# A hybrid mixer and mixture-of-experts layer on one core: two expert pairs in a fixed place instead of one, gathered together in front; the order of pairs and fours; the order of the routing steps; the sort key of the fixed experts

## The chip, the core and the metric

The kernel runs on one core of one Trainium2 chip. The time is device time in microseconds for one execution, from launch to the last output. Lower is better.

## What is computed

One decoder layer for 512 tokens of 1024 features, all in float32. The first half is a mixer: one input projection (1024 to 3072), a gated short convolution on one part, block attention on the other, an output projection, and a layer norm after the residual. The second half is a mixture of 32 experts in 4 groups, two experts for each token, plus a gated per-layer embedding ("PLE"), and a second layer norm. The reference, cut to what matters here:

```python
mix = jnp.concatenate([y_conv, y_attn], axis=-1) @ w_out[i]
x = layer_norm(DEEPNORM_ALPHA * x + mix, ln1_g[i], ln1_b[i])
# routing: one group of four by softmax, then two of its eight experts
g_p, g_idx = lax.top_k(softmax(xt @ w_router_g + b_router_g), 1)
e_p, e_local = lax.top_k(softmax(e_logits_of_that_group), 2)
weights = g_p * (e_p / e_p.sum(-1, keepdims=True))
# every expert, on the tokens that chose it (D_EXPERT = 512)
hid = silu(xb @ w_gate[e]) * (xb @ w_up[e])
y = y.at[tokens].add((hid @ w_down[e]) * weight)
ple = sigmoid(x @ w_ple_gate[i]) * (p[i] @ w_ple_proj[i])
x = layer_norm(DEEPNORM_ALPHA * x + y + ple, ln2_g[i], ln2_b[i])
```

The weights of the 32 experts are 192 MiB (201 MB) of float32 in HBM. Every one of them is read once in every execution.

## The kernel before

**The front.** The kernel does the mixer with float32 split into a high and a low part, three matmuls for one product (`mm3`, lines 132 to 134). Then comes the output projection of the four tiles of 128 tokens, tt = 0 to 3. `project(tt, half, part)` is 12 matmuls of 128x512; part 1 multiplies the attention's half, part 0 the convolution's. `residual`, `stats`, `centre_row`, `finish_row` and `low_row` make the layer norm of a tile on VectorE (with two tiny steps of GpSimd for the root), and leave it as a high part `x1h` and a low part `x1l`. `turn_raw` transposes a tile for the router, `logits` makes the router's 40 columns, `route` finds each token's two experts on VectorE (`mb` marks them), `rank` counts each token's place within its expert, `select` writes 0/1 matrices of tokens against places, and `gather_first` multiplies x1h and x1l by them, which collects the first unit's tokens in `xe[0]`. `router_constants` folds the norm's gain and bias into the router's weights.

**The table.** `sort_experts` orders the experts by their number of tokens, so that the fullest stand first. It writes `table` (line 712), the row in HBM where each sorted expert's weights begin. The first NFIX experts by number are kept out of the sorting: they always stand first, so that their weights can be fetched without the table.

**The units.** The sorted experts are worked through in 12 units, by `KINDS`. A "P" unit is a pair of experts with 64 places each, and its weights are 12 pieces of 1 MiB. A "Q" unit is four experts with 32 places each and has 24 such pieces. There are 8 P and 4 Q units. For a unit, TensorE does `gate_up` for k = 0 to 7, then `swiglu` (ScalarE and VectorE), `turn_hidden` (four transpositions), `down` for f = 0 to 3; `scatter_pair` adds the result to the tokens' rows while the next unit runs. Units are put together in `GROUPS`; during the last unit of a group the next group's tokens are gathered (`gather_group`, 8 pieces). The PLE's 16 tasks are spread over units by the dictionary `PLE`.

**The slots and the queue of loads.** SBUF holds 24 slots of 1 MiB (`Slots`, first in, first out). All loads stand in one queue in a fixed order; `pump` takes a slot for the next load wherever one has been given back. All DMAs are issued by SyncE (SP), one after another, and a load's issue waits until the last reader of its slot is done; what stands behind it waits too. An entry in `closed` stops the queue: `("e", 1, 0, 0)`, the first piece of unit 1, is closed until the table is written, because that load's address comes from the table (`load_expert`, line 263 reads the table, line 266 issues; line 258 issues the loads of unit 0, whose place is fixed). Towards the end `("e", 11, 0, 10)` holds back the last two pieces until `overflow` has run; that is a branch taken when some expert has more tokens than its unit has places.

```python
def pump(reserve, ahead=99):
    while queue and slots.left() > reserve and len(loaded) < ahead and queue[0][0] not in closed:
```

## Time and profile before

| | before |
|---|---|
| median of 3 runs | 785.05 us (784.99 to 785.3) |
| the profiled execution, its own time | 784.13 us |
| its span, first to last instruction | 782.3 us |
| granted clock of TensorE, mean | 0.980 |
| PE busy / weight load busy | 744.1 us (95%) / 449.6 us (57%) |
| VectorE / ScalarE / GpSimd busy | 311.0 / 164.1 / 73.5 us |
| moved by DMA | 233.53 MB, mean 299 GB/s |

The profiled execution stands 0.9 us below the median; its time is 1.8 us more than its span. Matmuls are pipelined and their ends are modelled, so that PE's busy share says little about how much room PE has. The share of the DMA engines is a mean over stages of different kinds.

### The profile page before, as it was taken

How to read it: one execution, taken by the hardware profiler on the slowest of the kernel's cores; microseconds unless marked ns; L12 is line 12 of the kernel's file. 1: busy time of each engine (PE TensorE's matmuls, PEld its weight loads, DVE VectorE, ACT ScalarE, POOL GpSimd, SP SyncE). 2: the span in 40 equal slices, each digit the busy share in tenths (PEclk: the TensorE clock that was granted, in tenths of full speed). 3: DMA queues.
4: the chain of work that ended last, by engine and by line, in shares of the span. 5: the costliest groups of instructions: out<-in, count | busy, mean ns of one | idle time of the engine just before them, and what ended most of it. 6: DMA issues, size and time to landing. Idle time of an engine off the chain costs nothing. (4 is left out here: it accounts for less than half of the span.)

```text
span 782.3 us, 11777 instructions
## 1 busy us (share of the span) xinstructions
PE 744.1 (95%) x4404; PEld 449.6 (57%) x4404; DVE 311.0 (40%) x646; ACT 164.1 (21%) x341; POOL 73.5 (9%) x104
## 2 busy tenths in 40 slices
PE   7999999999988899899999999999999999999995
PEld 4887877888866552247344653364454634447442
DVE  3746544746467513525440224241123333203254
ACT  5545444332011120103210120110010110001023
POOL 0224245000001000000000100000010000001005
PEclk9999999999989699999999999999999999999999
DMA  8500301547243998999999999998999999999952
GB/s 312 195 1 28 135 1 55 215 163 293 83 183 140 326 373 302 411 409 405 409 408 409 409 408 410 409 356 313 409 407 408 410 408 409 409 409 409 401 191 108
DMA packets 63708, 233.53 MB, mean 299 GB/s; under 512 B 7056, under 2 KB 10784, under 8 KB 59296
## 3 DMA queue, kind: packets, MB, share of 16 engines
q1 hardware_dynamic: 63648, 232.75, 76.0%
q8 instruction: 36, 0.59, 0.3%
q14 instruction: 24, 0.20, 0.1%
HBM read 230.62 MB, written 2.10 MB: 297 GB/s over the span
## 5 line engine op out<-in xcount | busy, mean ns | idle before, releaser
L983 PE MATMUL ps_mm<-big,big 128*32 128x512 f32 (+1 forms) x1024 | 215.5, 602 | 8.5 <-DMA big<-in_w_e_dram 7.7
L983 PEld LDWEIGHTS ps_mm<-big,big 128*32 128x32 f32 (+1 forms) x1024 | 57.8, 123 | 138.4 <-issue 85.7
L132 PE MATMUL ps_mm<-big,big 128*128 128x512 f32 (+1 forms) x240 | 91.2, 380 | 3.1 <-ACT big L118 3.1
L133 PE MATMUL ps_mm<-big,big 128*128 128x512 f32 (+1 forms) x240 | 88.6, 369 | 0.2 <-DVE big L119 0.2
L134 PE MATMUL ps_mm<-big,big 128*128 128x512 f32 (+1 forms) x240 | 88.3, 368 | 0.1
L1003 PE MATMUL ps_y<-big,ht 128*32 128x512 f32 (+1 forms) x480 | 84.2, 603 | 0.2 <-DMA big<-in_w_e_dram 0.2
L1024 DVE TENSOR_TENSOR big<-big,ps_s 128x512 f32<-128x512 f32 x80 | 52.9, 684 | 69.7 <-PE ps_s L1015 69.5
L119 DVE TENSOR_TENSOR big<-big,big 128x512 fp32r<-128x512 f32 (+1 forms) x74 | 58.3, 824 | 31.4 <-ACT big L118 26.5
L1015 PE MATMUL ps_s<-big,pt 128*128 128x512 f32 x176 | 59.4, 438 | 0.5 <-DVE big L1024 0.4
L118 ACT CAST big<-big 128x512 fp32r<-128x512 f32 (+1 forms) x74 | 50.5, 726 | 38.2 <-DVE big L432 20.1
L132 PEld LDWEIGHTS ps_mm<-big,big 128*128 128x128 f32 x240 | 46.4, 193 | 17.4 <-issue 6.7
L807 PEld LDWEIGHTS ps_s<-big,big 128*128 128x128 f32 x384 | 48.8, 190 | 9.8 <-issue 6.6
L801 POOL TENSOR_TENSOR big<-big,ps 128x256 f32<-128x256 f32 x16 | 11.7, 734 | 438.4 <-DVE ps L797 351.6
L807 PE MATMUL ps_s<-big,big 128*128 128x256 f32 (+1 forms) x384 | 51.9, 284 | 0.0
L134 PEld LDWEIGHTS ps_mm<-big,big 128*128 128x128 f32 x240 | 46.1, 192 | 8.0 <-DVE big L119 0.6
L133 PEld LDWEIGHTS ps_mm<-big,big 128*128 128x128 f32 x240 | 46.2, 193 | 7.3 <-DVE big L119 0.8
L1003 PEld LDWEIGHTS ps_y<-big,ht 128*32 128x32 f32 (+1 forms) x480 | 22.0, 123 | 41.4 <-issue 36.6
L374 POOL TENSOR_SCALAR big<-big,rden 128x128 f32<-128x128 f32 (+3 forms) x32 | 39.1, 1233 | 71.0 <-DVE rden L372 71.0
L797 DVE TENSOR_TENSOR ps<-ps,ps_s 128x256 f32<-128x256 f32 x16 | 6.7, 422 | 98.1 <-ACT ps L796 98.1
L1015 PEld LDWEIGHTS ps_s<-big,pt 128*128 128x128 f32 x176 | 29.3, 192 | 26.8 <-issue 17.3
L132 PE MATMUL ps_s<-big,big 128*128 128x256 f32 x128 | 37.4, 292 | 0.2
L133 PE MATMUL ps_s<-big,big 128*128 128x256 f32 x128 | 36.1, 282 | 0.0
(249 smaller groups left out, 811.0 us busy)
## 6 DMA issues: line engine op xcount, KB each, us to landing
big<-in_w_e_dram SPq DMA_DIRECT2D x360, 512.0 KB, 10.2
big<-in_w_e_dram SPq DMA_DIRECT2D x12, 1024.0 KB, 9.9
big<-in_w_in_dram SPq DMA_DIRECT2D x11, 1024.0 KB, 6.3
big<-in_w_out_dram SPq DMA_DIRECT2D x4, 1024.0 KB, 6.0
big<-in_w_pg_dram SPq DMA_DIRECT2D x4, 1024.0 KB, 11.1
big<-in_xtok_dram SPq DMA_DIRECT2D x2, 1024.0 KB, 6.9
out_dram<-big SPq DMA_DIRECT2D x8, 256.0 KB, 2.2
big<-in_xT_dram SPq DMA_DIRECT2D x3, 512.0 KB, 8.0
```

The costliest lines, as they stand in the source:

```text
L118: nc.scalar.copy(hi, raw)
L119: nc.vector.tensor_sub(lo, raw, hi.bitcast(F32))
L132: nc.tensor.matmul(o, ah, bh, start=first, stop=False)
L133: nc.tensor.matmul(o, ah, bl, start=False, stop=False)
L134: nc.tensor.matmul(o, al, bh, start=False, stop=last)
L374: nc.gpsimd.tensor_scalar(pr[h][:, 0:ks], pr[h][:, 0:ks], rden[:, h:h + 1], None, op0=ALU.mult)
L801: nc.gpsimd.tensor_tensor(r, r, s, op=ALU.add)
L807: nc.tensor.matmul(o[:, 0:n], src[tt // 2].t[:, tt % 2, k * P:(k + 1) * P], pt(tt), start=(i == 0), stop=(i == 2 * NT - 1))
L983: nc.tensor.matmul(o[a][i * m:(i + 1) * m], x, w[:, a * FE:(a + 1) * FE], start=(k == 0), stop=(k == KD - 1))
L1003: nc.tensor.matmul(o[h][r], ht[:, f, r], w[:, h * 512:(h + 1) * 512], start=(f == 0), stop=(f == 3))
L1015: nc.tensor.matmul(o, pt[0:m, tt * P:(tt + 1) * P], y[i][0:m], start=(i == 0), stop=(i == 1))
L1024: nc.vector.tensor_add(r, r, o)
```

## The change

Two constants and a table of kinds change: `KINDS` from "PQPPQPPQPPQP" to "PPPQPQPQPQPP", `NFIX` from 2 to 4, and `GROUPS` from [0], [1,2], ... [11] to [0,1], [2,3], ... [10,11]. Units 0 and 1 (experts 0 to 3) are now fixed, so 24 pieces of 1 MiB stand in the queue before the first that needs the table. `gather_first` collects the tokens of both units at once, 256 columns instead of 128, in four PSUM banks instead of two, and in more steps. `router_constants` is cut into three steps that stand between the projections; its 32 matmuls become 8 small ones and 2 that spread the result. `rank` and `select` of tiles 0 and 1 now come after tile 2's projection. `finish_row` and `low_row` of tile 2, and `finish_row` of tile 3, come before the last `route`; ten matmuls of zeros (`keep_warm`) stand behind the gather of tiles 0 and 1. The token weights, the rest of `sort_experts` and `rank(mc)` move into unit 0. The sort key of a fixed expert now also depends on its number, so that the four keep their order. `PLE` spreads the tasks as 5, 1, 4, 1, 5 over units 5 to 9 (before 4, 1, 5, 1, 5 over units 4, 6, 7, 9, 10).

```diff
--- before.py
+++ after.py
@@ -29,13 +29,13 @@
 CAP = 64
 NBLK = T // CAP
 SMALL = 32
-KINDS = "PQPPQPPQPPQP"
+KINDS = "PPPQPQPQPQPP"
 NU = len(KINDS)
-NFIX = 2
+NFIX = 4
 NWIDE = 2 * KINDS.count("P")
 UNITS = [(2 * KINDS[:u].count("P"), 2, CAP) if v == "P" else (NWIDE + 4 * KINDS[:u].count("Q"), 4, SMALL)
          for u, v in enumerate(KINDS)]
-GROUPS = [[0]] + [list(range(u, min(u + 2, NU))) for u in range(1, NU, 2)]
+GROUPS = [[u, u + 1] for u in range(0, NU, 2)]
 NP = NE // 2
 NG = len(GROUPS)
 GROUP_OF = {u: (g, r) for g, us in enumerate(GROUPS) for r, u in enumerate(us)}
@@ -49,7 +49,7 @@
 SEL = 1024.0
 N_SLOTS = 24
 WARM = 9
-PLE = {4: 4, 6: 1, 7: 5, 9: 1, 10: 5}
+PLE = {5: 5, 6: 1, 7: 4, 8: 1, 9: 5}
 WEIGHTS = {"P": [1.5, 0, 1.5, 0] + [5, 2.5] + [0, 1, 0], "Q": [2, 2, 2, 1.5] + [3, 2] + [1, 2, 1]}
 LAST = [4, 0, 4, 0, 2, 2]
 
@@ -136,7 +136,7 @@
 
     queue = deque()
     loaded = {}
-    closed = {("ln2",), ("e", 1, 0, 0), ("e", NU - 1, 0, 10)}
+    closed = {("ln2",), ("e", NFIX // 2, 0, 0), ("e", NU - 1, 0, 10)}
 
     def pump(reserve, ahead=99):
         while queue and slots.left() > reserve and len(loaded) < ahead and queue[0][0] not in closed:
@@ -254,8 +254,8 @@
 
     def load_expert(n, j, u, t):
 
-        if n == 0:
-            nc.sync.dma_start(t, w_e[0, u])
+        if 2 * n < NFIX:
+            nc.sync.dma_start(t, w_e[n, u])
             return
         for i in range(2):
             col = UNITS[n][0] + 2 * j + i
@@ -310,7 +310,8 @@
         gp.tensor_scalar(rowv[0:NE], evec[0:NE], ROWS / 2, None, op0=ALU.mult)
         gp.tensor_tensor(rowv[0:NE], rowv[0:NE], kcol[0:NE], op=ALU.add)
         for key, e in ((kcol, evec), (krow, eiota)):
-            gp.tensor_scalar(key[0:NE], e[0:NE], float(NFIX), FIRST, op0=ALU.is_lt, op1=ALU.mult)
+            gp.tensor_scalar(key[0:NE], e[0:NE], -1.0, float(NFIX), op0=ALU.mult, op1=ALU.add)
+            gp.tensor_scalar(key[0:NE], key[0:NE], 0.0, FIRST, op0=ALU.max, op1=ALU.mult)
             gp.tensor_tensor(key[0:NE], key[0:NE], e[0:NE], op=ALU.subtract)
         gp.tensor_scalar(caps, eiota, float(NWIDE), float(CAP - SMALL), op0=ALU.is_lt, op1=ALU.mult)
         gp.tensor_scalar(caps, caps, float(SMALL), None, op0=ALU.add)
@@ -609,20 +610,25 @@
                 nc.tensor.matmul(o[h, 0:NR], turned.t[:, tt % 2, k, h], wr[:, k], start=(k == 0), stop=(k == KD - 1))
         return o
 
-    def router_constants():
+    def router_constants(step):
 
         o = ps("z")
-        nc.tensor.transpose(o[:, 0:2 * KD], lnrows[0:2 * KD], ident[0:2 * KD, 0:2 * KD])
-        nc.vector.tensor_copy(gb, o[:, 0:2 * KD])
-        o = ps("z")
-        for i in range(2):
+        if step == 0:
+            nc.tensor.transpose(o[:, 0:2 * KD], lnrows[0:2 * KD], ident[0:2 * KD, 0:2 * KD])
+            nc.vector.tensor_copy(gb, o[:, 0:2 * KD])
+        elif step == 1:
             for k in range(KD):
-                nc.tensor.matmul(o[:, i * NR:(i + 1) * NR], gb[:, i * KD + k, None].to_broadcast([P, P]), wr[:, k],
+                nc.tensor.matmul(o[0:2, 0:NR], gb.rearrange("p (i k) -> p i k", i=2)[:, :, k], wr[:, k],
                                  start=(k == 0), stop=(k == KD - 1))
-        nc.vector.tensor_tensor(wr, wr, gb[:, 0:KD, None].to_broadcast([P, KD, NR]), op=ALU.mult)
-        nc.vector.tensor_scalar(gsum, o[:, 0:NR], -1.0 / D, None, op0=ALU.mult)
-        nc.vector.tensor_tensor(wr, wr, gsum[:, None, :].to_broadcast([P, KD, NR]), op=ALU.add)
-        nc.vector.tensor_add(br, br, o[:, NR:2 * NR])
+            nc.vector.tensor_copy(gsum[0:2], o[0:2, 0:NR])
+        else:
+            for i in range(2):
+                nc.tensor.matmul(o[:, i * NR:(i + 1) * NR], ident[0:2, i:i + 1].to_broadcast([2, P]), gsum[0:2],
+                                 start=True, stop=True)
+            nc.vector.tensor_tensor(wr, wr, gb[:, 0:KD, None].to_broadcast([P, KD, NR]), op=ALU.mult)
+            nc.vector.tensor_scalar(gsum, o[:, 0:NR], -1.0 / D, None, op0=ALU.mult)
+            nc.vector.tensor_tensor(wr, wr, gsum[:, None, :].to_broadcast([P, KD, NR]), op=ALU.add)
+            nc.vector.tensor_add(br, br, o[:, NR:2 * NR])
 
     gsum, lgr = work[:, 112:112 + NR], [work[:, 112 + NR * i:112 + NR * (i + 1)] for i in (1, 2)]
     wsp = cpool.tile([P, NT, NE, 2], F32R, name="wsp")
@@ -710,7 +716,7 @@
         o2 = ps("s")
         nc.tensor.matmul(o2[0:1, 0:NE], rowv[0:NE], hot[0:NE], start=True, stop=True)
         nc.vector.tensor_copy(table[0:1], o2[0:1, 0:NE])
-        closed.discard(("e", 1, 0, 0))
+        closed.discard(("e", NFIX // 2, 0, 0))
         yield
         q = qs.rearrange("p (a t) -> p a t", a=2)
         tmp = sm("ht", [P, 4, P], bufs=1)[:, 0].rearrange("p (t e) -> p t e", t=NT)
@@ -861,22 +867,27 @@
                 nc.vector.tensor_reduce(wsl[g][r][p, 0:1], o[p, c:c + 2], axis=AX.X, op=ALU.add)
         yield 0.05
 
-    def gather_first(tts, banks2=None, ks=range(KD)):
-        o = banks2
+    def gather_first(tts, o=None, ks=range(KD), srcs=(0, 1), end=False):
         if o is None:
-            o = [ps("mm") for _ in range(2)]
+            o = [ps(v) for v in ("mm", "mm", "y", "y")]
             for b in o:
                 nc.tensor.matmul(b, zerob, onesb[:, 0:1].to_broadcast([P, 512]), start=True, stop=False)
         for k in ks:
-            d = o[k // 4][:, (k % 4) * P:(k % 4 + 1) * P]
+            d = o[k // 2][:, (k % 2) * GROUP:(k % 2 + 1) * GROUP]
             for tt in tts:
-                for s in (x1h, x1l):
-                    nc.tensor.matmul(d, s[tt // 2].t[:, tt % 2, k * P:(k + 1) * P], picks(0, 0, tt),
-                                     start=False, stop=(k % 4 == 3 and tt == NT - 1 and s is x1l))
-            if k % 4 == 3 and tts[-1] == NT - 1:
-                (nc.scalar.copy if k == 7 else nc.vector.tensor_copy)(
-                    xe[0].t[:, k - 3:k + 1, 0:P], o[k // 4].rearrange("p (k s) -> p k s", k=4))
+                for i in srcs:
+                    last = end and k % 2 and tt == tts[-1] and i == srcs[-1]
+                    nc.tensor.matmul(d, (x1h, x1l)[i][tt // 2].t[:, tt % 2, k * P:(k + 1) * P], picks(0, 0, tt, 2),
+                                     start=False, stop=bool(last))
+            if k % 2 and end:
+                (nc.scalar.copy if k % 4 == 3 else nc.vector.tensor_copy)(
+                    xe[0].t[:, k - 1:k + 1], o[k // 2].rearrange("p (k s) -> p k s", k=2))
         return o
+
+    def keep_warm(o, n):
+
+        for i in range(n):
+            nc.tensor.matmul(o[i % 4], zerob, onesb[:, 0:1].to_broadcast([P, 512]), start=False, stop=False)
 
     def gather_group(g):
 
@@ -893,9 +904,11 @@
         for half in range(2):
             project(tt, half, 1)
             piece()
+            if tt == 0:
+                router_constants(half)
+    router_constants(2)
     while parts:
         piece()
-    router_constants()
     pump(2)
     for tt in range(2):
         for half in range(2):
@@ -923,18 +936,19 @@
     pump(4)
     lg[1] = logits(1)
     route((1, lg[1]))
-    rank(mb, 0, 2, NFIX)
-    select(0, (0, 1))
     project(2, 0, 0)
     residual(2, 0)
     project(2, 1, 0)
     residual(2, 1)
     stats(2)
+    rank(mb, 0, 2, NFIX)
+    select(0, (0, 1))
     project(3, 0, 0)
     turn_raw(2, 0)
     turn_raw(2, 1)
     centre_row(2)
     residual(3, 0)
+    finish_row(2)
     project(3, 1, 0)
     slots.give(ych, ycl, *(w[j] for j in (0, 1) for w in (woh, wol)))
     pump(2)
@@ -943,28 +957,27 @@
     residual(3, 1)
     turn_raw(3, 1)
     stats(3)
-    finish_row(2)
-    first = gather_first((0, 1), None, range(4))
+    low_row(2)
+    first = gather_first((0, 1), None, range(2))
     lg[3] = logits(3)
     centre_row(3)
+    finish_row(3)
     route((2, lg[2]), (3, lg[3]))
-    gather_first((0, 1), first, range(4, KD))
+    gather_first((0, 1), first, range(2, KD))
+    keep_warm(first, 10)
     rank(mb, 2, NT, NFIX)
     select(0, (2, 3))
     steps = sort_experts()
-    for _ in range(3):
-        next(steps)
-    low_row(2)
-    finish_row(3)
+    next(steps)
     low_row(3)
+    gather_first((2,), first)
+    next(steps)
+    next(steps)
     slots.give(ln1t, turned)
     pump(0)
-    gather_first((2, 3), first)
+    gather_first((3,), first, srcs=(0,))
+    gather_first((3,), first, srcs=(1,), end=True)
     weights = token_weights()
-    next(weights)
-    next(steps)
-    rank(mc, 0, NT, NE)
-    next(weights)
 
 
     def place(t, cols, n, cap):
@@ -1243,10 +1256,16 @@
                 add(7.7 if len(GROUPS[g + 1]) > 1 else 5.3, gather_group(g + 1))
             if k > 0:
                 chore()
-            if n == 0 and k == 2:
+            if n == 0 and k == 0:
+                next(weights)
+                next(steps)
+            if n == 0 and k == 1:
+                rank(mc, 0, NT, NE)
+                next(weights)
+            if n == 0 and k == 4:
                 late[0] = group_weights(0)
                 next(late[0])
-            if r == 0 and k == 4:
+            if r == 0 and k == 6:
                 for _ in late.pop(g):
                     pass
             if n == 2 and k == 6:
```

Three places show how the rows move. The first is the queue of SP's DMAs at the point where the table is first read; `big` is a slot, `in_w_e_dram` the experts' weights, 128x2048 a piece of 1 MiB. Before:

```order
L258 DMA big_2084<-in_w_e_dram 128x2048
L258 DMA big_2086<-in_w_e_dram 128x2048
L263 TENSOR_LOAD table
L263 ISA x2
L266 ISA
L266 DMA big_2253<-in_w_e_dram 128x1024
```

And of the change:

```order
L258 DMA big_2402<-in_w_e_dram 128x2048
L258 DMA big_2420<-in_w_e_dram 128x2048
L263 TENSOR_LOAD table
L263 ISA x2
L266 ISA
L266 DMA big_2426<-in_w_e_dram 128x1024
```

The read of the table stood behind 12 pieces of line 258 and now stands behind 24; nothing but such pieces lies between the 12th and the 24th.

The second place is VectorE where tile 2's projection ends. Line 655 (661 in the change) is the last step of tile 1's `route`, lines 687 to 830 (693 to 836) are `rank` and `select` of tiles 0 and 1, line 561 (562) is tile 2's residual, line 566 (567) its `stats`, line 572 (573) its `centre_row`. Before:

```order
L655 COPY lgs<-ps 128x4
L687 SCALAR_TENSOR_TENSOR rm<-mb,ps_s 128x2x2
L689 TENSOR_SCALAR rmb<-rm 128x2x2
L830 TENSOR_TENSOR big_2005<-cs,rm 128x128 x2
L561 SCALAR_TENSOR_TENSOR big_1581<-big_1581,ps_mm 128x512
L562 BN_STATS st<-big_1581 128x6
```

And of the change:

```order
L563 BN_STATS st<-big_1583 128x6
L567 BN_AGGR mv<-st 128x2
L693 SCALAR_TENSOR_TENSOR rm<-mb,ps_s 128x2x4
L695 TENSOR_SCALAR rmb<-rm 128x2x4
L836 TENSOR_TENSOR big_2038<-cs,rm 128x128 x4
L573 SCALAR_TENSOR_TENSOR big_1583<-big_1583,mv,big_1664 128x1024
L562 SCALAR_TENSOR_TENSOR big_1583<-big_1583,ps_y 128x512
```

`rank` and `select` stood between tile 1's `route` and tile 2's residual, and now stand behind tile 2's statistics; on PE the matmuls of `rank` (lines 685 and 686 of before) move in the same way from ahead of `project(2, 0, 0)` to behind `project(2, 1, 0)`.

The third place is VectorE at the end of the front. Lines 699 to 712 (705 to 718) are `sort_experts` up to the table, line 584 (585) is `low_row`, line 580 (581) `finish_row`, line 877 (883) the copy of the gathered tokens into `xe`. Before:

```order
L701 TENSOR_SCALAR gt<-ps,kc 32x32
L707 COPY pc<-ps_s 32x1
L708 TENSOR_SCALAR ps<-cs,pc 32x32
L712 CAST table<-ps_s 1x32
L584 TENSOR_TENSOR big_2125<-big_1581,big_2124 128x1024
L580 SCALAR_TENSOR_TENSOR big_1581<-big_1581,rs,big_1662 128x1024
L584 TENSOR_TENSOR big_2125<-big_1581,big_2124 128x1024
L877 COPY big_2003<-ps_mm 128x4x128
```

And of the change:

```order
L707 TENSOR_SCALAR gt<-ps,kc 32x32
L585 TENSOR_TENSOR big_2072<-big_1583,big_2071 128x1024
L713 COPY pc<-ps_s 32x1
L714 TENSOR_SCALAR ps<-cs,pc 32x32
L718 CAST table<-ps_s 1x32
L883 COPY big_2035<-ps_mm 128x512
L883 COPY big_2035<-ps_y 128x512
```

Three large steps stood between the table and the copy: `low_row(2)`, `finish_row(3)` and `low_row(3)`. Now `low_row(3)` alone is left, and it stands ahead of the table's last steps; the other two are done before the last `route`.

## Rows read from the trace of the kernel before

**Rows 1.** The page's transfer rate in 40 equal slices of 19.56 us.

```profile
GB/s 312 195 1 28 135 1 55 215 163 293 83 183 140 326 373 302 411 409 405 409 408 409 409 408 410 409 356 313 409 407 408 410 408 409 409 409 409 401 191 108
```

**Rows 2.** Windows: us; PE, PEld, DVE, ACT, POOL busy (count); clock; DMA; GB/s.

```profile
226.00:243.00 17.00, 15.71 (x87) 12.86 (x88) 8.53 (x21) 1.67 (x3) 0.74 (x2) 0.81 0.76 308
243.00:255.50 12.50, 8.06 (x105) 6.98 (x100) 10.01 (x44) 1.69 (x3) 2.59 (x2) 0.90 0.22 85
255.50:266.00 10.50, 8.67 (x44) 7.46 (x46) 5.20 (x19) 1.78 (x4) 0.29 (x1) 0.50 0.96 305
290.00:310.00 20.00, 20.00 (x144) 6.09 (x140) 4.99 (x12) 1.49 (x4) 0.00 (x0) 1.00 0.75 268
310.00:500.00 190.00, 182.79 (x1068) 87.68 (x1068) 67.73 (x134) 25.04 (x48) 2.93 (x4) 0.99 1.03 409
500.00:541.00 41.00, 40.80 (x236) 22.20 (x232) 13.91 (x25) 6.42 (x13) 0.73 (x1) 1.00 0.87 337
740.00:758.00 18.00, 17.44 (x91) 7.70 (x89) 7.67 (x16) 2.14 (x4) 0.00 (x0) 1.00 0.69 245
```

**Rows 3.** What SP's DMA queue waits for: line, releaser, total us, times, longest.

```profile
SPq L266 <- DMA big<-in_w_e_dram: 189.3, 253, 2.5
SPq L258 <- DVE big L584: 40.6, 1, 40.6
SPq L258 <- PE ps_y L134: 14.7, 1, 14.7
SPq L263 <- DVE table L712: 11.1, 1, 11.1
SPq L1047 <- SPq L1047: 9.9, 4, 6.9
```

**Rows 4.** Timeline of SP: start, us, line, tile, count.

```profile
224.66 17.32 SPq L258 DMA_DIRECT2D big<-in_w_e_dram  x6
254.10 45.93 SPq L266 DMA_DIRECT2D big<-in_w_e_dram  x34
```

**Rows 5.** Two windows of the front, columns as before.

```profile
195.90:202.70 6.80, 6.80 (x26) 5.53 (x27) 2.58 (x6) 0.00 (x0) 0.00 (x0) 0.81 0.53 219
254.00:264.50 10.50, 7.65 (x43) 7.24 (x43) 5.40 (x14) 1.25 (x2) 0.00 (x0) 0.50 0.84 255
```

**Rows 6.** Timeline of PE in the front; brackets: idle before, and its releaser.

```profile
191.89 4.20 PE L620 MATMUL ps_z<-pt,gb 128*128 128x40 f32 x32 [0.27 <-DVE gb L616]
...
227.29 0.16 PE L686 MATMUL ps_s<-mb,marks 128*128 128x2 bf16 x1 [3.90 <-DVE mb L654]
...
246.22 1.13 PE L609 MATMUL ps_z<-pt,big 128*64 128x40 f32 x32
...
254.27 0.48 PE L874 MATMUL ps_mm<-big,big 128*128 128x128 f32 x1 [1.15 <-DVE big L584]
256.54 0.47 PE L874 MATMUL ps_mm<-big,big 128*128 128x128 f32 x1 [1.79 <-ACT big L581]
```

**Rows 7.** Timeline of VectorE at the end of the front.

```profile
249.88 0.41 DVE L654 SCALAR_TENSOR_TENSOR mb<-cs,jf,hw 128x32 bf16<-128x32 f32 x2
...
252.91 0.18 DVE L712 CAST table<-ps_s 1x32 int32<-1x32 f32 x1 [0.40 <-PE ps_s L711]
253.01 1.20 DVE L584 TENSOR_TENSOR big<-big,big 128x1024 fp32r<-128x1024 f32 x1
```

**Rows 8.** Timeline of PE in the first units.

```profile
264.48 4.75 PE L983 MATMUL ps_mm<-big,big 128*64 128x512 f32 x16
...
279.48 3.65 PE L983 MATMUL ps_mm<-big,big 128*64 128x512 f32 x16
283.06 4.11 PE L807 MATMUL ps_s<-big,big 128*128 128x256 f32 x32
...
309.57 0.73 PE L1015 MATMUL ps_s<-big,pt 128*128 128x512 f32 x2
```

**Rows 9.** The page's DMA issues: tile, queue, count, KB, median us to landing.

```profile
big<-in_w_e_dram SPq DMA_DIRECT2D x12, 1024.0 KB, 9.9
```

## The prediction

> **What bounds the kernel now.** I read the page's transfer rate first. From the seventeenth slice to the last but two it stands at 401 to 411 GB/s in all but two slices; before them lies the front, in which it swings between 1 and 373 [rows 1]. A window of 190 us in the middle gives 409 GB/s and a DMA share of 1.03 [rows 2]. So the middle of the kernel is a stream of expert weights, at 409 GB/s or 2.564 us for 1 MiB (1,048,576 bytes by 409 GB/s). 192 MiB take 492 us of it. What SP waits for agrees: 189.3 us in 253 waits go to the landing of earlier loads, and only single waits go to an engine [rows 3]. PE looks as full in that window (182.79 of 190 us), but its matmuls overlap the weights' arrival, and weight loading takes only 87.68 us; I count PE's own work below and find it shorter than the stream.
>
> The kernel can therefore gain in two ways: start the stream earlier, or take out places where it does not run. I add the places up from the windows [rows 2], each as its length by the share of 409 that is missing: 226 to 243, 4.2 us; 243 to 255.5, 9.9 us; 255.5 to 266, 2.7 us; 290 to 310, 6.9 us; 500 to 541, 7.2 us; 740 to 758, 7.2 us. Together 38.1 us. The first three have one reason: after 12 MiB the queue needs the table. SP sends the first six pieces of unit 0 early, then waits 40.6 us for a slot, then 14.7 us for another, then 11.1 us for the table [rows 3]. The pieces 7 to 12 leave between 224.66 and 241.98, the table's loads from 254.10 [rows 4]; the table itself is written at 252.91 [rows 7].
>
> **The front, part by part.** The 32 matmuls of the router's constants take 4.20 us on PE [rows 6]. Ten remain, 8 of them no wider than those; at 4.20/32 = 0.13 us each that is 1.3 us at most, and I take 0.7: 3.5 us gained, bounds 2.9 and 4.2. Behind them PE runs 6.80 us at a granted 0.81 [rows 5]. That is 1.2 GHz for part of the window and 2.4 GHz for the rest; with the row of little matmuls gone, full speed would do the same in 5.5 us. I take 1.3, bounds 0 and 1.3. So tile 1's logits, and the slots that tile 1's `low_row` and the attention's last projection give back, come 4.9 us earlier. Piece 7 leaves at about 219.8 instead of 224.66.
>
> Then PE waits 3.90 us for `mb`, the marks of tiles 0 and 1 [rows 6]. In the change `rank` stands behind tile 2's projection, some 5.5 us of matmuls later, so the wait is covered; what is queued behind it, `project(2)` and `project(3)`, starts at once. From 226 to 243 the granted clock was 0.81 [rows 2]: 17 by 0.19 is 3.2 us. I give that back too, since the idle stretch ahead of the slow part goes; the low bound is 0. The convolution's last projection, which frees six slots at 241.98 [rows 4], then ends at 241.98 − 4.9 − 3.9 − 3.2 = 230.0 (bounds 229 and 235).
>
> A matmul of 512 columns takes 3.65/16 = 0.228 us and one of 256 columns 4.11/32 = 0.128 [rows 8]. Between 230 and the table PE has: 32 gather matmuls of 256 columns, 4.1 us; 14 matmuls of zeros, 3.2 us; two logits of 1.13 [rows 6]; some 1.2 us of half turns; `rank` and sorting, 1.0 us, with 3.0 us of VectorE's steps from `mb` at 249.88 to the table at 252.91 [rows 7]; under 1 us of switches. The sum, 15.8 us, puts `low_row(3)` at about 246. The big step of 1.20 us that followed the table [rows 7] and its neighbours of the same size now lie under PE's logits. Adding tile 3's 16 gather matmuls (2.05 us) and the copies (0.7 us), unit 0 starts at 249.5, where it started at 264.48 [rows 8]: 15 us earlier.
>
> **The stream after the change.** It now has 24 pieces that need no table. 18 slots are free without any unit; the other six hold x1h and x1l (4), `xe` and one of the PLE's. Pieces 7 to 9 leave at 219.8 and are through by 229; pieces 10 to 15 leave at 230.0, and their data flow from 231.5, an idle of 2.5 us. From there the flow has to be kept fed. Six pieces last 15.4 us, to 246.9; piece 16 needs the slot that `low_row(3)` frees at 246, by 245.5: 0.5 us lost. Pieces 17 and 18 get theirs beside it. Piece 19 needs unit 0's first eight matmuls, at 250.9; it is wanted at 253: 2 us of margin. Unit 0 is 48 matmuls of 0.228, 10.9 us, with 3.2 us of activation and turning and 2.4 us of waits: 16.5 us against 30.8 us in which the stream brings 12 MiB. Unit 1 has the same, with 8 scatter steps of 0.73 us [rows 8] and 64 gather matmuls of 0.128 us: 28 us, and ends near 294. The last slot held over from the front is wanted at 304. So SP does not run dry in front.
>
> The losses from 290 to 310 and from 500 to 541 both fall behind a pair's unit (0 and 6) that ends its group, and so gathers the next one's tokens while it gives back only 12 slots, late. With groups [0,1], [2,3] and so on, the second to the fifth end in a unit of four, which gives back 24. Counted through the order of slots taken and given, I find never fewer than six loads ahead, where before it was five in the sixth unit. I give both stalls back, 6.9 and 7.2 us; low bound 0 for the second. PE's own work in the units is 12 by about 14 us, 64 us of scatter, 44 of gather, 62 of PLE and 7 of turns: 345 us against 470 of stream, which leaves it out as a bound.
>
> The end keeps its shape: both orders close with pairs, and the last two pieces wait until `overflow`'s branch is past [rows 3]. The 7.2 us of 740 to 758 and all behind them stay.
>
> **The sum.** Before: 38.1 us of missing stream. After: 2.5 + 0.5 + 7.2, and 0.5 us for the joints, 10.7 us. The stream starts 4.9 us earlier. 4.9 + 38.1 − 10.7 = 32.3 us. The profiled execution, 784.13 us, would be 751.8; the median stands 0.9 above it, so **753**. As bounds: with the front's clock and router terms at their low ends and the second stall kept, 753 + 2 + 3.2 + 7.2 = 765.4; with the 2.5 us of idle gone, the joint free and the end a little shorter, 747.
>
> **The rivals.** The first: the stream is unbroken, but the front comes late. For it speaks the clock in the last stretch of routing, 0.50 from 254 to 264.5 [rows 5], which is 1.2 GHz throughout, after PE had waited 1.15 us for `low_row`'s step and 1.79 us for another [rows 6]. If the stretch from 242 to 264 of before kept that pace in the change, `low_row(3)` and unit 0 would be 4 to 12 us later, and the queue would run dry for as long: 757 to 764. Against it: ten matmuls of zeros fill one of those waits, and the windows at 1.00 begin as soon as a unit runs.
>
> The Trainium skill, page "TensorE: Matmul & The Clock Gate", section "HAM oscillation — how this bites in real kernels", says that batches of matmuls with idle gaps between them each start at the low clock again. The trace agrees: 0.81 around the 3.90 us wait, 0.50 in the stretch from 254 to 264.5. By that rule the new stretch from 232 to 249, whose batches are still short, could stay slow, which is this rival's time.
>
> The second: a new stall in the middle or in front. Three pairs in a row now stand first, and unit 5 takes five of the PLE's tasks with their slots. A stall of the measured size, 7.2 us, gives 760. Against it speaks the count of six.
>
> The third: the change does not do what it says. The pieces of unit 1 may stand in the queue but find no slots, because `xe` now holds two units' tokens and x1h and x1l stay held until the gather's end. Then the stream waits for unit 0, and only PE's 15 us are won: 769.5. Against it: 18 slots are free by the order of the two programs, of which only three are needed behind the attention's projection.
>
> The fourth, on the other side: an expert with more than 32 tokens stands in a place of 32. Which experts do is set by the sorting, and now four, not two, are exempt; each of them takes a wide place whatever its count. If one expert too many is pushed out, `overflow` runs with its loads one after another. Six pieces of 1 MiB at 9.9 us to landing [rows 9] are about 60 us: 753 + 60 = 813, slower than before. It decides from the first such expert on. Counting the reference's routing on its inputs, the fixed four hold 33, 29, 32 and 40 tokens and the fullest behind the sixteen wide places has 32: no overflow, but with nothing to spare.
>
> The fifth: PE becomes the bound. 345 us of work would need a granted clock below 345/470 = 0.73; the rows show 0.99 and 1.00.
>
> **How the numbers follow.** The forecast, 750 to 757 as its own range: 0.62. The late front: 0.13. A new stall: 0.13. No slots: 0.06. Overflow: 0.04. PE as the bound or something else not seen, of unknown sign: 0.02. The range must leave out no more than 0.2: 747 to 766 takes in the first three with most of their tails and leaves out the last three, 0.12, and some of the second. About 0.2%, 1.6 us, is what can be told from no change here. Only the overflow and half of the unseen end above 785 for sure; I add 0.01 for no change: faster 0.94, same 0.01, slower 0.05.
>
> **What would show it.** 24 issues of line 258, the seventh near 220 and the tenth near 230; no wait of PE for `mb` ahead of tile 2's projection, and a granted clock of 1.00 from 195 to 230; `low_row(3)` near 246 and unit 0's first matmul at 249 to 250; no slice of the rate below 400 between 232 and the end, except the last two pieces; the last weights landed near 725. The forecast is wrong if the clock falls to 0.5 between 232 and 249, if SP waits over 3 us for an engine between pieces 10 and 40 or in a unit that gathers, or if work of line 1047's branch appears.

## The result, and the profile after

The changed kernel takes 771.48 us (median of 4 runs, 770.63 to 773.77) against 785.02 us (median of 4, 781.54 to 785.3): 0.9842 of the time before, 95% interval 0.9806 to 0.9878. That is 13.5 us faster. The forecast was 753, with 747 to 766 as the range, so the sign was right and the gain less than half of what was said. The profiled execution is the slowest of the four, 773.77 us with a span of 772.0.

The page's transfer rate, in 40 slices of 19.3 us, answers to [rows 1]:

```profile
GB/s 296 218 1 1 164 1 55 152 228 223 161 161 332 410 296 340 368 410 409 407 409 408 387 401 345 383 409 408 407 404 391 409 408 408 410 407 408 388 169 109
```

The forecast was a rate without a dip from 232 us on. The trough of [rows 1] ahead of slice 14 is filled, but slices 15 to 17 (270 to 328 us) stand at 296, 340 and 368, and slices 23 to 26 (425 to 502) at 387, 401, 345 and 383. The windows of the changed kernel, columns as in [rows 2], give the sizes:

```profile
223.00:235.00 12.00, 11.94 (x89) 9.73 (x87) 10.12 (x28) 1.51 (x3) 0.88 (x2) 1.00 0.75 275
235.00:254.00 19.00, 14.60 (x137) 11.86 (x139) 12.30 (x51) 3.71 (x6) 2.53 (x2) 1.00 0.94 382
254.00:270.00 16.00, 15.21 (x92) 5.05 (x88) 6.25 (x28) 2.60 (x6) 0.29 (x1) 1.00 1.01 424
270.00:320.00 50.00, 48.05 (x252) 23.10 (x252) 19.76 (x38) 5.70 (x13) 0.00 (x0) 0.97 0.88 323
320.00:420.00 100.00, 95.35 (x588) 44.62 (x588) 40.09 (x82) 16.11 (x28) 0.00 (x0) 0.98 1.03 409
420.00:500.00 80.00, 77.00 (x497) 41.41 (x494) 18.85 (x36) 8.95 (x19) 3.67 (x5) 1.00 0.99 380
500.00:730.00 230.00, 225.03 (x1318) 112.10 (x1317) 61.35 (x123) 21.11 (x45) 8.11 (x11) 1.00 1.03 406
730.00:746.00 16.00, 12.00 (x57) 4.96 (x54) 4.07 (x6) 2.14 (x4) 0.00 (x0) 0.84 0.75 263
```

Worked out as in the prediction (length by the share of 409 that is missing), the stream loses 10.5 us from 270 to 320, 5.7 us from 420 to 500, 1.7 us from 500 to 730 and 5.7 us at the end. The granted clock is 1.00 from 223 to 270, where it was 0.81, 0.90 and 0.50 [rows 2].

SP tells who holds the loads back. The waits of SP's queue in the changed kernel, 250 to 320 us (line, releaser, total, times, longest):

```profile
SPq L266 <- PE ps_mm L996: 12.1, 8, 4.1
SPq L258 <- PE ps_mm L996: 11.6, 5, 4.2
SPq L266 <- PE ps_y L1016: 10.4, 2, 8.7
SPq L266 <- PE ps_s L1028: 6.6, 1, 6.6
```

These are the four longest of seven; none of the seven is for an earlier load to land, and all are for PE: line 996 is `gate_up`, 1016 `down`, 1028 `scatter`, the last readers of slots. In the kernel before, 264 to 320 us, the largest was for loads:

```profile
SPq L266 <- DMA big<-in_w_e_dram: 14.8, 17, 2.2
SPq L266 <- PE ps_y L1003: 10.8, 1, 10.8
```

The timeline of PE in unit 0 and at the start of units 1, 2 and 3 (start, us, count) answers to [rows 8]:

```profile
253.41 3.65 PE L996 MATMUL ps_mm<-big,big 128*64 128x512 f32 x16
...
258.30 5.32 PE L996 MATMUL ps_mm<-big,big 128*64 128x512 f32 x24
...
264.12 3.65 PE L996 MATMUL ps_mm<-big,big 128*64 128x512 f32 x16
...
267.92 1.94 PE L996 MATMUL ps_mm<-big,big 128*64 128x512 f32 x8
...
272.61 8.78 PE L1016 MATMUL ps_y<-big,ht 128*64 128x512 f32 x32 [0.68 <-ACT ht L1009]
281.23 3.60 PE L996 MATMUL ps_mm<-big,big 128*64 128x512 f32 x16
...
315.49 3.65 PE L996 MATMUL ps_mm<-big,big 128*64 128x512 f32 x16
...
344.20 3.64 PE L996 MATMUL ps_mm<-big,big 128*32 128x512 f32 x32
```

Unit 0 starts at 253.41, 11.1 us earlier than before and 3.9 later than forecast. It has 16 + 24 + 16 + 8 = 64 matmuls of line 996 and 32 of line 1016: 96, not 48. The program has 32 calls of `gate_up` and 16 of `down` for a pair; each call with these float32 weights leaves two matmuls in the trace. Unit 0 takes 27.8 us to the start of unit 1, and unit 1, which also gathers and scatters, 34.3 us (315.49 - 281.23). Unit 3, of four experts, has matmuls of 32 rows, twice as many at half the time each (32 in 3.64 us): the same work for PE as a pair, for twice the weights. In the 30.8 us of stream that belong to a pair PE has little room.

The loads themselves leave as the change says. The timeline of SP (start, us, count):

```profile
222.67 43.75 SPq L258 DMA_DIRECT2D big<-in_w_e_dram  x18
267.81 51.54 SPq L266 DMA_DIRECT2D big<-in_w_e_dram  x34
```

With the six sent early these 18 make the 24 fixed pieces. Piece 7 leaves at 222.67 (219.8 was forecast), pieces 10 to 15 from 233.24 (230.0), piece 16 at 249.8 (246). Then comes the stop: by the issue times in this trace pieces 26 and 27 leave at 269.9 and 279.7, and piece 28 at 284.9. The single wait of 8.7 us on `down` stands there.

### The profile page after: what moved, and what is told of

It reads as the page before. It is cut to its first block, busy times and chain, and to the rows that moved or that the text cites. A ratio compares the mean times of both kernels' runs of the same rounds, so it can differ in the third digit from the quotient of the medians.

```text
span 772.0 us, 11569 instructions
## 1 busy us (share of the span) xinstructions
PE 733.3 (95%) x4340; PEld 436.8 (57%) x4340; DVE 309.1 (40%) x644; ACT 163.2 (21%) x338; POOL 74.0 (10%) x106
## 5 line engine op out<-in xcount | busy, mean ns | idle before, releaser
L996 PE MATMUL ps_mm<-big,big 128*64 128x512 f32 (+1 forms) x1024 | 215.6, 602 | 10.5 <-DMA big<-in_w_e_dram 9.3
L996 PEld LDWEIGHTS ps_mm<-big,big 128*64 128x64 f32 (+1 forms) x1024 | 57.9, 123 | 143.0 <-issue 85.3
L1028 PE MATMUL ps_s<-big,pt 128*128 128x512 f32 x176 | 57.8, 432 | 0.7 <-DVE big L1037 0.6
L813 PEld LDWEIGHTS ps_s<-big,big 128*128 128x128 f32 x320 | 41.3, 189 | 5.9 <-issue 3.3
L813 PE MATMUL ps_s<-big,big 128*128 128x256 f32 x320 | 43.8, 285 | 0.0
L132 PE MATMUL ps_s<-big,big 128*128 128x256 f32 x128 | 37.0, 289 | 0.1
L133 PE MATMUL ps_s<-big,big 128*128 128x256 f32 x128 | 36.2, 282 | 0.0
L134 PE MATMUL ps_s<-big,big 128*128 128x256 f32 x128 | 36.1, 282 | 0.0
```

The source lines that it names most:

```text
L132: nc.tensor.matmul(o, ah, bh, start=first, stop=False)
L133: nc.tensor.matmul(o, ah, bl, start=False, stop=False)
L134: nc.tensor.matmul(o, al, bh, start=False, stop=last)
L813: nc.tensor.matmul(o[:, 0:n], src[tt // 2].t[:, tt % 2, k * P:(k + 1) * P], pt(tt), start=(i == 0), stop=(i == 2 * NT - 1))
L996: nc.tensor.matmul(o[a][i * m:(i + 1) * m], x, w[:, a * FE:(a + 1) * FE], start=(k == 0), stop=(k == KD - 1))
L1028: nc.tensor.matmul(o, pt[0:m, tt * P:(tt + 1) * P], y[i][0:m], start=(i == 0), stop=(i == 1))
```

## The experiments

Two theories stood against each other. A: from unit 0's start to about 320 us every slot is taken, and loads leave only as fast as PE gives slots back; so the time hangs on when PE starts and how fast it works, not on when addresses are known. B: the early loads are the gain, and the loss behind 270 is a thing of its own. All edits are to the changed kernel, and ratios are to the kernel before on the same chip.

**Holding unit 1's pieces back in the program (e1).**

```diff
-    closed = {("ln2",), ("e", NFIX // 2, 0, 0), ("e", NU - 1, 0, 10)}
+    closed = {("ln2",), ("e", 1, 0, 0), ("e", NU - 1, 0, 10)}
...
-        closed.discard(("e", NFIX // 2, 0, 0))
+        closed.discard(("e", 1, 0, 0))
```

> The changed kernel with one thing undone: the pieces of unit 1 again wait until the table is written, though they need nothing from it. They leave at about 252 instead of 234.6 to 250, which idles the stream for some 10 us (243 to 253). Theory A (from unit 0's start to about 320 us no slot is free, and loads leave as PE gives slots back): the 10.6 us that the changed kernel loses between 270 and 320 shrink by nearly the same amount, and the time is 771 to 775 us. Theory B (the early loads are the gain, and the loss behind 270 is a separate one): 10 us more, 780 to 783 us.

772.26 us (ratio 0.9846, 0.9806 to 0.9886). The edit did not do what was expected of it, so it tells nothing between A and B. The pieces' instructions moved in the program, but SP had nothing to wait for ahead of them, and the trace has all 18 behind the early six as before, beginning at 221.44:

```profile
221.44 45.26 SPq L258 DMA_DIRECT2D big<-in_w_e_dram  x18
```

**Unit 1's addresses from the table (e5)**, which makes them truly wait:

```diff
-        if 2 * n < NFIX:
+        if n == 0:
             nc.sync.dma_start(t, w_e[n, u])
```

(with the entry of `closed` as in e1).

> The changed kernel, but the 12 pieces of unit 1 get their addresses from the table (the experts are the same, since they are sorted to the front), so that they truly wait for it. In the run before, the pieces were only held back in the program's order; they read nothing from the table, and left as before. Now pieces 13 to 18 should leave behind 252 us instead of 234.6 to 250.7, and the stream stands for some 9 us ahead of it. Theory A (behind unit 0's start the slots, not the addresses, are short): the loss from 270 to 320, 10.6 us in the changed kernel, shrinks by about as much, 771 to 775 us. Theory B (the early pieces are the gain): 780 to 784 us.

773.41 us (0.9867, 0.9833 to 0.9901), 1.9 us above the changed kernel, which the spread of the runs does not tell from nothing. SP and the windows:

```profile
222.02 11.85 SPq L258 DMA_DIRECT2D big<-in_w_e_dram  x6
253.30 46.70 SPq L266 DMA_DIRECT2D big<-in_w_e_dram  x40
```

```profile
240.00:253.00 13.00, 11.56 (x108) 9.91 (x108) 6.18 (x40) 0.55 (x1) 0.00 (x0) 0.88 0.13 53
270.00:320.00 50.00, 47.90 (x253) 22.58 (x250) 19.91 (x37) 6.12 (x14) 0.00 (x0) 0.97 1.03 409
```

Piece 13 leaves at 253.30 instead of 234.6, the stream stands still from 240 to 253 (53 GB/s, 11.3 us lost), and nearly all of it comes back: from 270 to 320 the rate is 409 instead of 323. Theory A holds and B falls: the early addresses of the second pair, taken by themselves, are worth 1.9 us by the medians, if anything.

**Shorter units (e6).** Part of the products is left out:

```diff
-    def gate_up(o, k, xs, ws):
+    def gate_up(o, k, xs, ws, cut=False):
+        c = FE // 2 if cut and k else FE
...
-                nc.tensor.matmul(o[a][i * m:(i + 1) * m], x, w[:, a * FE:(a + 1) * FE],
+                nc.tensor.matmul(o[a][i * m:(i + 1) * m, 0:c], x, w[:, a * FE:a * FE + c],
...
-                    [b.t[:, i] for b in bs for i in range(2)])
+                    [b.t[:, i] for b in bs for i in range(2)], n < 3)
```

> The changed kernel with part of the work left out: in units 0 to 2 the gate and up products of k = 1 to 7 are done for 256 of their 512 columns. That takes some 6.4 us of TensorE from each of the three units and changes no load and no slot. Theory A (behind unit 0's start loads leave as TensorE gives slots back): the loss from 270 to 320 shrinks from 10.6 to 2 to 4 us, 761 to 765 us. Theory C (only the five slots that unit 0 turns over to other tiles make the loss, whatever the pace): 769 to 772 us.

763.01 us (0.9739, 0.9707 to 0.9771), 8.5 us below the changed kernel, in the middle of what A gives. The window:

```profile
270.00:320.00 50.00, 47.79 (x311) 27.14 (x308) 24.85 (x58) 5.72 (x13) 0.00 (x0) 0.99 1.02 403
```

323 has become 403 GB/s, by PE's pace alone; no slot and no load was changed. C, by which only the slots that are turned over count, falls as a cause of its own.

**One slot less (e8)**, `N_SLOTS = 23`.

> The changed kernel with 23 slots instead of 24. Theory A (the stream's losses are a want of slots): one slot less is one piece less ahead when unit 0 turns slots over to other tiles, 2.6 us more in the front, and some more where the PLE's chunks hold slots: 774 to 779 us. Rival (the losses are TensorE's pace alone): 771 to 773 us.

785.04 us (1.0021, 1.0001 to 1.0041): 13.6 us, the whole gain of the change, and nearly twice what I expected at most. The windows:

```profile
270.00:320.00 50.00, 47.90 (x253) 22.70 (x250) 19.92 (x37) 5.96 (x14) 0.00 (x0) 0.97 0.88 329
320.00:420.00 100.00, 93.98 (x580) 44.86 (x580) 40.23 (x82) 16.11 (x28) 0.00 (x0) 0.97 1.02 405
420.00:500.00 80.00, 74.86 (x478) 39.02 (x474) 15.88 (x33) 8.95 (x19) 3.67 (x5) 1.00 0.96 361
500.00:730.00 230.00, 223.06 (x1295) 110.13 (x1296) 60.58 (x120) 21.11 (x45) 8.10 (x11) 1.00 1.01 399
```

In front the rate is the same as with 24 (329 and 323), since there loads leave at PE's pace whatever their number; the 2.6 us that I expected there do not show. The loss comes later: 405 against 409 from 320 to 420 (1.0 us), 361 against 380 from 420 to 500 (3.7), 399 against 406 over the next 230 us (3.9), the latter two in the units with PLE tasks. That is 8.6 us, as much as lies between the two profiled executions (782.07, the fastest of ten, and 773.77, the slowest of four: 8.3); where the rest of the 13.6 between the medians goes, no profile shows. The middle of the changed kernel, which has 6 pieces ahead at the least by my count, has no slot to spare.

**The third and fourth unit changed over (e7)**, `KINDS = "PPQPPQPQPQPP"`.

> The changed kernel with its third and fourth unit changed over, so that two pairs stand in front and then four experts, and the second group ends with a pair. Theory A (the loss lies in units 0 and 1, and a pair that ends a group costs some of its own): no gain, 770 to 776 us. Theory D (three pairs in a row are what the stream cannot follow): 762 to 766 us.

773.53 us (0.9867, 0.9837 to 0.9897). The rate from 270 to 320 is 323, as in the changed kernel:

```profile
270.00:320.00 50.00, 47.90 (x269) 22.58 (x266) 19.93 (x37) 6.01 (x14) 0.00 (x0) 0.97 0.90 323
```

D falls: what the stream loses there is settled in units 0 and 1.

**The front alone (e3) and the rest alone (e4).** e3 has the old `KINDS`, `GROUPS`, `NFIX` and `PLE` with the new front (the gather takes 128 columns, and `rank(mc)` follows k = 0); e4 keeps those of the change and puts the routing steps and the router's constants (still the cheaper ones) back in their old places:

```diff
-KINDS = "PPPQPQPQPQPP"
-NFIX = 4
+KINDS = "PQPPQPPQPPQP"
+NFIX = 2
...
-            d = o[k // 2][:, (k % 2) * GROUP:(k % 2 + 1) * GROUP]
+            d = o[k // 2][:, (k % 2) * GROUP:(k % 2) * GROUP + P]
```

```diff
     route((1, lg[1]))
+    rank(mb, 0, 2, NFIX)
+    select(0, (0, 1))
     project(2, 0, 0)
...
-    keep_warm(first, 10)
...
     rank(mb, 2, NT, NFIX)
     select(0, (2, 3))
     steps = sort_experts()
...
+    for _ in range(3):
+        next(steps)
+    low_row(2)
+    finish_row(3)
     low_row(3)
```

> The new order of the front alone: one fixed pair, the old order of units, the old groups and the old spread of the PLE, with the changed kernel's routing order, router constants and matmuls of zeros. Unit 0 starts near 251 instead of 264.5 and the table is written near 250 instead of 252.9. Theory A (what counts is when TensorE begins to give slots back): the loss of 6.9 us from 290 to 310 goes as well, and the time is 772 to 777 us. Theory B (what counts is when loads can be issued): only the table's 3 us and the earlier first pieces count, 779 to 782 us.

> The two fixed pairs, the new order of units, the groups and the spread of the PLE, with the old order of routing: router constants in one place, rank and select of tiles 0 and 1 ahead of tile 2's projection, low_row of tile 2 and finish_row of tile 3 behind the table, token weights ahead of unit 0, no matmuls of zeros. Unit 0 starts near 266. Theory A (what counts is when TensorE begins to give slots back): 782 to 787 us, next to nothing is left. Theory B (the early loads are the gain): 774 to 778 us.

e3: 779.02 us (0.9934, 0.9914 to 0.9954; 776.17 to 782.25 over 10 runs). e4: 782.39 us (0.9974, 0.9955 to 0.9994; 776.97 to 784.02). So the front alone gives 5.4 us, the rest alone 2.1, both together 13.5. e5, which has both but not the early addresses, gives 10.3 on its own chip. How much of the 6 us beyond the sum of the parts comes of their being together is not shown, since both parts alone had the clock fall in the front. e4 lies where A put it, e3 on the edge of B, but for a reason that neither foresaw: in its profile, the slowest of its ten runs, unit 0 did not start at 251 but at 258.89, since the clock fell:

```profile
240.47 1.71 PE L610 MATMUL ps_z<-pt,big 128*64 128x40 f32 x32 [2.88 <-DVE ps L649]
...
258.89 3.10 PE L996 MATMUL ps_mm<-big,big 128*64 128x512 f32 x8
```

```profile
240.00:250.00 10.00, 9.53 (x63) 7.83 (x64) 3.30 (x29) 1.05 (x1) 0.00 (x0) 0.54 0.23 98
```

e3's and e4's runs scatter over 6 and 7 us, and the faster ones have the higher mean clock (e4: 776.97 us at 0.986, 782 to 784 at 0.975 to 0.977; e3: 776 to 777 at 0.986 to 0.988, 780 to 782 at 0.979 to 0.980). The profile of e4 is its fastest run, so its unit 0's start (262.3) can't be put beside its median. How much of the 2.1 us belongs to the order of units stays open.

**The PLE's chunks one at a time (e2)**, `PLE = {5: 4, 6: 1, 7: 5, 8: 1, 9: 5}`.

> The changed kernel with the PLE's tasks as 4, 1, 5, 1, 5 over units 5 to 9, so that unit 4 claims slots for one chunk of the PLE's weights, not for two. Theory A (the 5.8 us lost between 430 and 490 come from the slots that two chunks hold at once): the rate stays above 400 there and the time is 765 to 768 us. Theory B (TensorE's work in unit 5 is too long): most of it moves to unit 7, which now has five tasks, and the time is 770 to 773 us.

773.27 us (0.9863, 0.9828 to 0.9899). The windows:

```profile
420.00:500.00 80.00, 74.92 (x462) 38.28 (x460) 19.84 (x36) 9.47 (x18) 2.94 (x4) 1.00 1.00 385
500.00:730.00 230.00, 223.70 (x1332) 113.92 (x1332) 60.43 (x122) 21.51 (x46) 8.82 (x12) 1.00 1.02 401
```

From 420 to 500 the rate is 385 instead of 380, from 500 to 730 401 instead of 406: 1.0 us less is lost in the first window and 2.8 more in the second. A falls. Of B only half is seen: a loss came to where the fifth task went, but most of unit 5's stayed.

**A third of the PLE's gate (e12).** Two of its three products are left out:

```diff
-            mm3(o[:, 0:256], xh[:, k, ts], xl[:, k, ts], gh[:, k], gl[:, k], k == 0, k == KD - 1)
+            nc.tensor.matmul(o[:, 0:256], xh[:, k, ts], gh[:, k], start=(k == 0), stop=(k == KD - 1))
```

> The changed kernel with part of the work left out: the PLE's gate does one of its three products (high by high), which takes about two thirds of its matmuls from units 5 to 9 and changes no load and no slot. Theory A1 (the loss of 5 to 6 us from 420 to 500 is TensorE's pace in units with PLE tasks, which gives slots back too late): the rate stays at 405 or more from 420 to 500, 764 to 767 us. Theory A2 (it is the slots alone that the PLE's weights hold): no change, 770 to 773 us.

768.28 us (0.9795, 0.9768 to 0.9822), 3.2 us below the changed kernel. The windows:

```profile
420.00:500.00 80.00, 76.04 (x428) 32.92 (x424) 18.85 (x36) 8.94 (x19) 3.66 (x5) 1.00 1.03 408
500.00:730.00 230.00, 216.99 (x1130) 91.95 (x1130) 61.50 (x123) 21.09 (x45) 8.06 (x11) 0.99 1.01 402
```

The loss from 420 to 500 is gone (408). In the changed kernel SP's longest waits there are for PE's `gate_up` and for loads:

```profile
SPq L266 <- PE ps_mm L996: 19.5, 8, 4.7
SPq L266 <- DMA big<-in_w_e_dram: 14.0, 18, 1.5
```

So PE's work sets the pace there too; some is given back behind 500 (402 instead of 406), which is why the time is a little above A1's range.

**No matmuls of zeros (e10); finish_row later as well (e11, e13).** In the changed kernel VectorE and PE wait for each other in the last stretch of routing:

```profile
247.01 0.16 DVE L693 SCALAR_TENSOR_TENSOR rm<-mb,ps_s 128x8 f32<-128x8 bf16 x1 [2.42 <-PE ps_s L692]
```

```profile
240.43 1.13 PE L610 MATMUL ps_z<-pt,big 128*64 128x40 f32 x32 [2.77 <-DVE ps L649]
...
246.22 0.60 PE L890 MATMUL ps_mm<-onesb,zerob 128*128 128x512 bf16 x2
246.65 0.19 PE L691 MATMUL ps_s<-mb,onesb 128*128 128x4 bf16 x2
```

The zeros (line 890) stand ahead of `rank` (691) on PE, while the marks have been ready since 244.4. And tile 3's logits wait for the one bank `ps_z`, which `route`'s first step (649) reads behind `finish_row` of tile 3.

```diff
     gather_first((0, 1), first, range(2, KD))
-    keep_warm(first, 10)
```

and, for e11 on top of it:

```diff
-    finish_row(3)
     route((2, lg[2]), (3, lg[3]))
+    finish_row(3)
```

In e13 `finish_row(3)` stands behind `select(0, (2, 3))` instead.

> The changed kernel without the ten matmuls of zeros. In its profile the marks of tiles 2 and 3 are ready at 244.4 us, the gather of tiles 0 and 1 ends at 244.6, and TensorE begins to count them only at 246.7, behind the zeros; VectorE waits 2.42 us for that. Theory A (the time follows unit 0's start): without a fall of the clock unit 0 starts 2.2 us earlier, near 251.2, and the time is 768.5 to 770.5 us. Rival (the zeros hold the clock): the granted clock between 244 and 254 falls below 0.9, unit 0 starts at 253 or later, and the time is 771 to 776 us.

> As the run without zeros, and finish_row of tile 3 stands behind the last route instead of ahead of it. In the changed kernel TensorE waits 2.77 us for tile 3's logits, because the one bank that logits use is read by route's first step, which stands behind finish_row on VectorE. Theory A: logits of tile 3 start some 1.5 us earlier, finish_row falls into a gap, unit 0 starts at 249.5 to 251, 3 us or so earlier than in the changed kernel, and the time is 767 to 770 us. Rival (the front no longer counts, since the stream is held by units 4 and 5 anyway): 771 us.

> The changed kernel without the matmuls of zeros and with finish_row of tile 3 behind the last select instead of ahead of the last route. In the run with finish_row right behind the last route, TensorE waited 1.68 us for the select that stood behind it. The time follows unit 0's start at about 1.2 us for each us, by the runs so far. If TensorE's wait shrinks to 0.8 and nothing else is late, unit 0 starts near 249 and the time is 765.5 to 767.5 us. Rival: low_row of tile 3, now 1 us later, is waited for by the last gather and by piece 16, and the time is 767 to 769 us.

e10: 770.11 us (0.9818, 0.9792 to 0.9843). e11: 767.14 us (0.9783, 0.9760 to 0.9805). e13: 767.62 us (0.9775, 0.9749 to 0.9800). e10's and e11's PE:

```profile
240.84 1.13 PE L610 MATMUL ps_z<-pt,big 128*64 128x40 f32 x32 [2.77 <-DVE ps L649]
...
251.62 3.65 PE L995 MATMUL ps_mm<-big,big 128*64 128x512 f32 x16
```

```profile
238.24 1.13 PE L610 MATMUL ps_z<-pt,big 128*64 128x40 f32 x32 [1.04 <-DVE ps L649]
...
244.56 1.22 PE L880 MATMUL ps_mm<-big,big 128*128 128x256 f32 x8 [1.68 <-DVE big L836]
...
249.94 3.65 PE L995 MATMUL ps_mm<-big,big 128*64 128x512 f32 x16
```

Unit 0 starts at 251.62 and 249.94 instead of 253.41, and the clock stays at 1.00 without the zeros (e10's window):

```profile
240.00:250.00 10.00, 7.78 (x96) 7.33 (x97) 6.87 (x42) 1.05 (x1) 0.00 (x0) 1.00 1.02 428
```

e10's runs have no lower mean clock than the changed kernel's (0.983 to 0.989 in both). e10's 1.4 us are within the spread, so for it alone the gain is not settled; e11's 4.3 us are more than that, and e11 beats both kernels. In e13 the wait for `select` shrank as hoped, but the table came later (PE waits 1.75 us for line 714, which stands behind `low_row`) and unit 0 started at 252.0 in its profile, with the clock low from 250 (four of the last gathers took 1.05 us instead of 0.64); its median is that of e11, though, so its rival (767 to 769) is what it shows.

Over the nine profiled executions with two pairs in front, 24 slots and all of the work (the changed kernel, e1, e2, e4, e5, e7, e10, e11, e13), unit 0's start runs from 249.9 to 262.3 and the execution's own time from 767.1 to 777.0, with a slope of 0.8 us for each us by least squares and up to 2.5 us of scatter. The slope hangs on e4, whose start lies 7 us behind the next: without it the other eight give 1.6. So an earlier start pays, and what one us of it is worth is not settled better than 0.8 to 1.6; the 1.2 that stands in an expectation paired starts of one execution with medians of others.

## Why the prediction was wrong

**The front: right in kind, 3.9 us short.** The wait of 3.90 us for `mb` is gone and the clock is at 1.00 in this execution, as forecast. The router's constants were mis-sized: I gave 0.7 us to what remains. The trace has three pieces with switches between them and a wait of 0.76 us:

```profile
188.18 0.74 PE L621 MATMUL ps_z<-pt,gb 128*2 128x40 f32 x16 [0.76 <-DVE gb L618]
...
194.53 0.63 PE L626 MATMUL ps_z<-ps,cs 2*128 2x40 f32 x4
```

The ten calls that remain are twenty matmuls, as the 32 of [rows 6] were 16 calls; I set calls against matmuls. From the start of the stretch ahead (144.93 before, 145.91 after) to the projection behind them (195.89 and 195.10), 1.8 us were won instead of 3.5. Another 1.0 us of delay was already there at 145.91, ahead of all that the forecast counted. (3.5 and 1.3 make 4.8, not 4.9; and the terms named between 230 and unit 0 make 248.6, not 249.5.) Of the three losses that I put down to the table, that from 226 to 243 was a wait for a slot (14.7 us for `ps_y` [rows 3]); it is still there, 3.9 us from 223 to 235 where I had 2.5. Piece 7 left 2.0 us earlier instead of 4.9, unit 0 started 11.1 us earlier instead of 15.

**The stream after the change: the step that failed.** "Unit 0 is 48 matmuls of 0.228, 10.9 us ... 16.5 us against 30.8 us in which the stream brings 12 MiB" took half of the matmuls. 48 is the number of calls in the program; 0.228 us is the time of one matmul in the trace [rows 8], and a call with float32 weights leaves two. A pair's unit has 64 for `gate_up` and 32 for `down`, 21.9 us, and 27.8 us in all; I never added up a whole unit in the trace. Units 0 and 1 together need 62.1 us, which is what the stream needs for their 24 pieces (61.5). The sign that I had named, a wait of SP of over 3 us for an engine between pieces 10 and 40, came with the 8.7 us behind piece 26. So SP has no lead that could grow, and each slot that goes elsewhere is a hole. e6 shows it: with some 6 us of PE's work taken from each of three units the rate is 403.

**The loss of [rows 2] from 290 to 310 was put down to the wrong thing.** I read it as that of a pair that ends its group, and gave back 6.9 us. The wait of 10.8 us for `ps_y` shown above is that of the first piece that gets a slot from unit 0's `down`. In both programs the slots of `down` f = 0 and 1 go to `acc`, that of f = 3 to `y`: of unit 0's last four slots one brings a load. In the change the next slot, unit 1's first, goes to the next group's tokens. The loss was not given back but grew to 10.5 us, since the loads had run up against the slots before unit 0 began. My margin for "the last slot held over" left `acc` and `y` out.

**From 420 to 500** the forecast was no loss, for the 7.2 us of 500 to 541 before. There are now 5.7, in unit 5 with its five tasks, where [rows 2] had 409 GB/s. "PE's own work in the units is 12 by about 14 us", 345 us, fell with the same count: 12 by 22 are 264 us and, with the scatter, gather, PLE and turns named there, 441 us of 470. e12 shows PE's work as the cause, e8 the want of slots as what lets it through.

**The sum, again.** 32.3 us were forecast. The late piece 7 takes 2.9 off. The losses up to the landing of the last weights, at 745.0, are 27.2 us instead of 10.7: 16.5 more. The tail behind that landing takes 2.5 us longer, 27.0 of a span of 772.0 where it was 24.5 (757.8 of 782.3), and the clock was low in it:

```profile
740.00:748.00 8.00, 6.08 (x22) 3.27 (x24) 1.06 (x3) 0.37 (x1) 0.00 (x0) 0.57 0.76 268
```

32.3 - 2.9 - 16.5 - 2.5 = 10.4, which is 784.13 - 773.77.

**The rivals.** The one whose time came nearest is the third, "only PE's 15 us are won: 769.5", with 0.06; that is in part luck, since PE won 11 us and not 15. Its place was wrong (the early pieces did find slots), its mechanism, a stream that waits for unit 0, right one unit later. The fifth, PE as the bound, had 0.02 because of the count. The late front by its clock did not come true in this execution, but e3's profile shows it: 0.54 from 240 to 250, and unit 0 at 258.89, 5.5 us later than in the changed kernel, within the 4 to 12 that I had put to it. The Trainium skill, page "TensorE: Matmul & The Clock Gate", section "HAM oscillation — how this bites in real kernels", says that a batch of matmuls behind a long enough wait starts at the low clock again. e3 agrees (2.88 us of waiting, then 1.71 us for logits that take 1.13 at full speed); the changed kernel and e10 kept full speed behind 2.77 us. No overflow block ran.

## What to carry to other kernels

Before you move loads forward, count a whole unit of the consumer: every matmul of it, by the rows of the trace and not by the program's calls, against the time in which its weights arrive. If the two are equal, buffers handed to other tiles are holes in the stream, early loads fill the buffers sooner and stop there, and what pays is to start the consumer earlier (e11: 3.5 us earlier in its profile, 4.3 us less by the medians) or to make its unit shorter (e6). A loss seen in the trace has to be tied to the instruction that held the buffer, by the queue's own waits, before it is given back in a forecast.

## What the hardware showed that was not expected

A float32 call of the program leaves two matmuls in the trace (32 calls of `gate_up`, 64 of line 996), a call on operands written as fp32r, such as those of the gather, one (64 calls of `gather_first`, 64 of line 880).

The same wait of PE ahead of tile 3's logits, 2.76 to 2.78 us, was followed by full speed in some profiled executions and not in others, though PE's work up to there is the same in all of them: the logits took 1.13 us in the changed kernel, e7, e8, e10 and e12, and 1.28 to 1.94 us in e1, e2, e5 and e6, whose mean granted clock from 235 to 254 is 0.91 where that of the others is 1.00. e1's:

```profile
239.20 1.94 PE L610 MATMUL ps_z<-pt,big 128*64 128x40 f32 x32 [2.76 <-DVE ps L649]
```

In e3, with a wait of 2.88 us and matmuls of 128 columns instead of 256 around it, the mean was 0.54 from 240 to 250, most of it at 1.2 GHz. e3's and e4's runs, which lie 6 and 7 us apart on one chip, go with their mean granted clock (0.979 to 0.988 and 0.975 to 0.986). So part of what one kernel's runs differ by is this clock; what decides it in a single execution, no run here tells.
